# Two hybrid decoder layers on one core: the trunk kept by token instead of by channel

## The chip, the cores and the metric

One NeuronCore of a Trainium2 chip runs the whole program. The metric is device microseconds of one execution. TensorE (PE) multiplies, with a separate record for each load of its stationary operand (PEld); VectorE (DVE), ScalarE (ACT) and GpSimd (POOL) work on vectors; SyncE (SP) issues most DMAs. Products land in PSUM, in banks of 128 partitions by 512 float32.

## The reference

256 tokens of 1024 channels pass through two layers. Each layer is an FFN, a mixer of three attention groups, and a second FFN, each added to the trunk `h`:

```python
for l in range(DEPTH):
    h = h + 0.5 * swiglu(rms_norm(h, ffn1_norm[l]), ffn1_w_gate[l], ffn1_w_up[l], ffn1_w_down[l])
    h = h + hybrid_mixer(rms_norm(h, mix_norm[l]), w_in[l], ...)
    h = h + 0.5 * swiglu(rms_norm(h, ffn2_norm[l]), ffn2_w_gate[l], ffn2_w_up[l], ffn2_w_down[l])
```

`swiglu(x) = (silu(x @ w_gate) * (x @ w_up)) @ w_down` has 2816 hidden channels. The mixer projects the normed trunk once, splits the result into heads of A (four heads over keys that a token indexer selects), B (four heads, causal) and C (eight heads with forget gates), rotates A's and B's queries and keys (rope), and multiplies the heads' outputs by `w_out`.

## The kernel before, in words

**Numbers in two parts.** Each weight and each activation is kept as a high part (rounded to the type fp32r) and a low part (what is left), and a product is made of three: high by high, high by low, low by high (`mm3`, L299). Weights come from HBM in 1 MB raw tiles of five rotating buffers on SP's queue; ACT casts each unit of 1024 columns to the high part (`wh`, L117) and DVE subtracts to get the low part (`wl`, L121). `Weights.pump` (L93) does one such unit ahead of its use; `take` (L133) hands out the next unit, and makes its low part at that point if it isn't there. At most seven units stand ready.

**Order.** The scheduling is by hand: each engine runs its instructions in the order in which the Python code issues them. An engine waits only where a semaphore tells that data or a buffer isn't ready.

**Layout of the trunk.** `hres` (L294) holds the trunk by channel: 128 partitions are channels, in eight slices of 256 tokens. `Norm` (L311) makes from each slice the operand `xhl` with the gains applied: `high` on ACT (L320), `low` on DVE (L323). The squares are taken by ACT (L327), added by POOL and DVE, and summed over partitions by a small TensorE product against ones (`sums`, L341). The root of the mean, by token, is made on POOL (`rsqrt`, L304), turned into a row by a TensorE product (`broadcast`, L348) and multiplied in later, behind the gate products.

**FFN** (L360). In rounds of 128 hidden channels, 22 of them: a gate and an up product (`pair`, L424: each holds 8 weight slices of 128x128 and moves 512 columns of high and low tokens, then 256 of high tokens), then sum, silu and product on ACT and DVE (`summed`, `gated`, `silu`, `hidden`, L439 to L468), which leave the hidden tile as `hh` and `hl`. Four rounds later comes the down product of that tile (`down`, L363). It holds a 128x128 block of weights and moves 256 tokens: 24 products for each hidden tile, into four PSUM banks `acc`, each with two channel slices. The last FFN differs: `turn_trunk` (L381) first transposes the trunk to token by channel, and `down_tokens` (L375) holds 128 tokens of the hidden tile and moves 512 weight columns, 12 products for each hidden tile; `finish` (L391) adds, and stores.

**Boundaries.** `tail` (L518) does the last four hidden tiles (or, in the mixer, the last three head pairs) bank by bank. Behind each bank come the residual addition on DVE (`residual`, L355), and the next norm's highs, lows and squares for its two slices, while TensorE goes on with the next bank. The next FFN begins with a pair in two groups of slices (six, then two), the sums, and the second pair with the broadcast between its wide and narrow products.

**Mixer** (L581). Eight projection chunks of up to 512 columns, each in four steps of two channel slices; they hold tokens and move weight columns. After each step, side work that is due by a step number runs (`at_step`, `run_side`, L585 to L592): rotation, transposes, the indexer, top-k, and B's heads. `post_a` (L800), called behind step 16, evacuates A's chunk and rotates its queries and key on POOL (`rope`, L597); A's root is due at step 22, its split at 24, its transposes at 26. For B's heads (`run_heads`, L917 on) `scores` and `exps` run in one step, `flip` two steps later, which transposes the probabilities and copies them to `pT`, `values` three steps later. A's and C's heads come behind the chunks, with half steps of the output product (`out_halves`) put between their parts.

**Start.** `x` is loaded into `xin`, which takes one of the five raw buffers, turned by TensorE, and the first FFN's first gate product is made slice by slice as it arrives; the turned trunk is then copied to `hres` by ACT and DVE.

Of the kernel before, what the change touches and what calls it, by code (L numbers as in the profile page):

```python
# [18 lines left out]
P = 128  # L19
# [20 lines left out]
B_TURN, B_STEP, A_ROOT, A_TURN, SUMS_STEP = 18, 20, 22, 26, 29  # L40
# [101 lines left out]
def kernel(ctx: ExitStack, tc: tile.TileContext, x, ffn1_norm, ffn1_w_gate, ffn1_w_up, ffn1_w_down,  # L142
# [24 lines left out]
    xin = raw_pool.tile([P, 2048], F32, name="xin", tag="raw").rearrange("p (t d) -> p t d", t=2)  # L167
# [18 lines left out]
    def load_x(mp):  # L186
        cols = slice(256 * mp, 256 * mp + 256)
        nc.sync.dma_start(xin[:, :, cols], x[0].rearrange("(t p) d -> p t d", p=P)[:, :, cols])
# [17 lines left out]
    W.n_raw_done = -1  # L206

# [56 lines left out]
    W.n_raw_done -= RAW_BUFS - 3  # L264
# [8 lines left out]
    W.n_raw_done += RAW_BUFS - 3  # L273
# [20 lines left out]
    hres = xp.tile([P, KT, S], F32, name="hres")  # L294
# [16 lines left out]
    class Norm:  # L311


        def __init__(self, which, l):
            self.col = 16 * which + 8 * l
            self.x = xp.tile([P, KT, 2, S], F32R, name="xhl", tag="xhl")
            self.h, self.l = self.x[:, :, 0], self.x[:, :, 1]
            self.acc = xp.tile([P, 2, S], F32, name="ssacc", tag="ssacc")

        def high(self, m, src=None):  # L320
            A.activation(self.h[:, m], hres[:, m] if src is None else src, AF.Copy, scale=gT[:, self.col + m:self.col + m + 1])

        def low(self, m, src=None):  # L323
            V.scalar_tensor_tensor(self.l[:, m], hres[:, m] if src is None else src, gT[:, self.col + m:self.col + m + 1],
                                   self.h[:, m].bitcast(F32), op0=ALU.mult, op1=ALU.subtract)

        def squares(self, mp):  # L327
            src = hres[:, 2 * mp:2 * mp + 2]
            if mp == 0:
                A.activation(self.acc, src, AF.Square)  # L330
                return
            sq = tmp(512).rearrange("p (a b) -> p a b", a=2)
            A.activation(sq, src, AF.Square)  # L333
            if mp < 3:
                G.tensor_tensor(self.acc, self.acc, sq, op=ALU.add)  # L335
            else:
                V.tensor_tensor(sq[:, 0], sq[:, 0], sq[:, 1], op=ALU.add)
                V.tensor_tensor(sq[:, 0], sq[:, 0], self.acc[:, 0], op=ALU.add)
                V.tensor_tensor(self.acc[:, 0], sq[:, 0], self.acc[:, 1], op=ALU.add)
# [15 lines left out]
    def residual(acc, m, n, factor):  # L355
        V.scalar_tensor_tensor(hres[:, m:m + n], acc[m // 2].rearrange("p (a b) -> p a b", a=2)[:, m % 2:m % 2 + n],
                               factor, hres[:, m:m + n], op0=ALU.mult, op1=ALU.add)


    def ffn(norm, nxt, aside=None, g0=None):  # L360
        hid = {}

        def down(k):  # L363
            w = W.take()
            if nxt is None:
                for j in range(4):
                    down_tokens(j, k, w, slice(0, 512), k == 0, False)
                del hid[k]
                return
# [5 lines left out]
        def down_tokens(j, k, w, cols, start, stop, o=None):  # L375

            t, c = divmod(j, 2)
            mm3(acc[j][:, cols] if o is None else o, [h[:, t * P:(t + 1) * P] for h in hid[k]],
                [v[:, 0, 512 * c + cols.start:512 * c + cols.stop] for v in w], start, stop)

        def turn_trunk():  # L381

            ps = [bank("acc") for _ in range(4)]
            for j in range(4):
                for i in range(4):
                    t, m = j // 2, 4 * (j % 2) + i
                    T.transpose(ps[j][:, i * P:(i + 1) * P], hres[:, m, t * P:(t + 1) * P], ident)
            for j in range(4):
                (A.copy if j % 2 else V.tensor_copy)(trunk[:, j], ps[j])

        def finish(ks):  # L391
            ws = [(k, W.take()) for k in ks]
            dst = out[0].rearrange("(t p) (c d) -> p t c d", p=P, c=2)

            def add(j, cols, ps):
                V.scalar_tensor_tensor(trunk[:, j, cols], ps, 0.25, trunk[:, j, cols], op0=ALU.mult, op1=ALU.add)

            for j in range(4):
                for c in ((0, 512),) if j < 3 else ((0, 256), (256, 512)):
                    c = slice(*c)  # L400
                    o = bank("gu")[:, :S] if c.start else acc[j][:, c]
                    if c.start:
                        add(j, c, acc[j][:, c])
                    for k, w in ws:
                        down_tokens(j, k, w, c, c.start > 0 and k == ks[0], k == ks[-1], o)
                    add(j, c, o)
                    nc.sync.dma_start(dst[:, j // 2, j % 2, c], trunk[:, j, c])

        trunk = hres.rearrange("p a b -> p (a b)").rearrange("p (j c) -> p j c", j=4)
# [14 lines left out]
        def pair(groups=(range(KT),), between=None):  # L424

            ws = [W.take() for _ in range(2)]
            pss = [bank("gu").rearrange("p (a b) -> p a b", a=2) for _ in range(2)]
            for ks in groups:
                for w, ps in zip(ws, pss):
                    for k in ks:  # L430
                        mm(ps, w[0][:, k], norm.x[:, k], k == 0, False)
                if between:
                    between()
                for w, ps in zip(ws, pss):
                    for k in ks:
                        mm(ps[:, 0], w[1][:, k], norm.h[:, k], False, k == KT - 1)
            return pss
# [33 lines left out]
        if first:  # L471
# [4 lines left out]
            for mp in range(1, 4):  # L476
                V.tensor_copy(hres[:, 2 * mp:2 * mp + 2], xT[mp])
# [16 lines left out]
        if nxt is None:  # L494
            turn_trunk()
        acc = [bank("acc") for _ in range(4)]
        for f in range(1, NF):
            last = f == NF - 1
            paired = f >= (PAIR_FROM if first else 2)
            if paired:  # L500
                g, u = pair()
# [16 lines left out]
    def tail(acc, rhs, ks, factor, make_norm, late=None):  # L518


        nxt = make_norm()
        ws = dict(zip(ks, [W.take() for _ in ks]))

        def part(mp, some):
            for k in some:
                for m in (2 * mp, 2 * mp + 1):
                    mm3(acc[mp][:, (m % 2) * S:(m % 2 + 1) * S], [v[:, 0, m * P:(m + 1) * P] for v in ws[k]],
                        rhs[k], False, k == ks[-1])
# [11 lines left out]
        for mp in range(4):  # L540
            ms = (2 * mp, 2 * mp + 1)
            part(mp, ks[ahead[mp]:])
            for m in ms:
                if mp == 3:
                    residual(acc, m, 1, factor)
                elif m == ms[0]:
                    residual(acc, m, 2, factor)
                nxt.high(m)
            if late and mp == 0:
                continue  # L550
            for m in ((0, 1) if late and mp == 1 else ()) + ms:
                nxt.low(m)
            for p in (([0] if late and mp == 1 else []) + ([mp - 1] if mp > 1 or (mp == 1 and not late) else [])
                      + ([3] if mp == 3 else [])):
                nxt.squares(p)
# [25 lines left out]
    def mixer(l, norm, nxt):  # L581
# [218 lines left out]
        def post_a(ps):  # L800
# [5 lines left out]
            for t in range(2):  # L806
# [110 lines left out]
        def run_heads(hs, qk, tag, emit=None, lag=1):  # L917
# [81 lines left out]
            for i, (kind, h) in enumerate(hs):  # L999
                emit(i - 0.5, lambda i=i: (scores(i), exps(i)))  # L1000
# [104 lines left out]
    def turn_x(mp):  # L1105
        ps = bank("acc").rearrange("p (m s) -> p m s", m=2)
        for t in range(2):
            for i in range(2):
                T.transpose(ps[:, i, t * P:(t + 1) * P], xin[:, t, (2 * mp + i) * P:(2 * mp + i + 1) * P], ident)
        xT.append(ps)  # L1110
# [41 lines left out]
    sq = []  # L1152
    for mp in range(4):
        sq.append(norm.acc if mp == 0 else tmp(512).rearrange("p (a b) -> p a b", a=2))
# [52 lines left out]
```

## Time and profile before

| | |
|---|---|
| median of 3 runs | 1053.11 us (1052.83 to 1054.24) |
| profiled execution | 1052.83 us |
| its span, first to last instruction | 1051.0 us |
| granted TensorE clock | 0.999 |
| HBM read | 179.67 MB, 172 GB/s over the span |
| VectorE's largest group, `wl` (L121) | 415.9 us busy, 343 instructions |
| ScalarE's largest group, `wh` (L117) | 345.2 us busy, 343 instructions |

The profile is of one execution. A row of a timeline or of the chain of waits gives the start in us, the time in us, the engine, line and operation with `out<-in`, the shapes (partitions x elements) and how many instructions the row merges; a bracket at its end is idle time of the engine before it, with what ended it. A row of grouped instructions ends in `xcount | busy us, mean ns of one | idle us before them, and what ended it`. A row of waits gives us in total, times and the longest. A row of stretches gives the stretch, its length, then busy us and instructions of PE, PEld, DVE, ACT and POOL, the granted clock, the DMA share and GB/s. Ends of products are modelled, and neighbours overlap; their starts are what the queue shows.

### The profile page before, as it was taken

The page shows a single profiled execution, that of the slowest core. Times are in us where ns is not written, and L with a number is a line of the kernel's source. Part 1 is how long each engine was busy: PE and PEld are TensorE (multiplying, and loading weights), DVE is VectorE, ACT ScalarE, POOL GpSimd, SP SyncE. Part 2 cuts the span into 40 slices and gives each one's busy share as a digit, 9 for nine tenths or more (in the row PEclk, how much of TensorE's full clock was granted, in tenths as well). Part 3 has the DMA queues.
Part 4 walks back from the last instruction along what each step waited for, and adds up shares of the span by engine and source line. Part 5 has one row for each costly group of instructions (what it writes and reads, how often), then busy time and mean ns, then how long its engine had stood idle before and what let it go on. Part 6 is the DMA issues. An engine that isn't in the chain of part 4 may idle for free.

```text
span 1051.0 us, 16911 instructions
## 1 busy us (share of the span) xinstructions
PE 1044.8 (99%) x6611; PEld 948.9 (90%) x6611; DVE 825.6 (79%) x1560; ACT 589.5 (56%) x1026; POOL 162.0 (15%) x184
## 2 busy tenths in 40 slices
PE   9999999999999999999999999999999999999998
PEld 8999999998899899999999999999988998888887
DVE  6997777889876887777788777777898779777775
ACT  6655454666854655454466545546667555554541
POOL 2003000167700100000010210003765000000000
PEclk9999999999999999999999999999999999999999
DMA  9675555365441374555646564645555215564631
GB/s 326 209 240 173 196 197 177 127 218 193 137 148 42 120 241 163 199 182 179 201 161 211 160 238 148 214 145 207 163 181 180 81 41 173 189 232 148 221 120 41
DMA packets 130912, 181.81 MB, mean 173 GB/s; under 512 B 7008, under 2 KB 104720, under 8 KB 130832
## 3 DMA queue, kind: packets, MB, share of 16 engines
q1 hardware_dynamic: 130512, 180.65, 51.5%
q8 instruction: 52, 0.85, 0.3%
q14 instruction: 28, 0.23, 0.1%
q10 hardware_dynamic: 320, 0.08, 0.0%
HBM read 179.67 MB, written 1.05 MB: 172 GB/s over the span
## 4 chain that ended last, share of the span: by engine, by line
PE 93%; DVE 3%; ACT 2%; DMA 1%; issue 0%; SPq 0%; ACTq 0%; DVEq 0%
PE ps_gu L297 61%; PE ps_acc L297 30%; DVE wl L121 1%; ACT wh L117 1%; DMA raw<-in_ffn_w_gate_dram 1%; PE ps_gu L953 1%; PE ps_gu L1053 0%; ACT tmp L615 0%; DMA xin<-in_x_dram 0%; DVE score L754 0%; PE ps_gu L986 0%; DVE tmp L939 0%; DVE tmp L1157 0%; DVE bkT L662 0%; ACT cka L630 0%
## 5 line engine op out<-in xcount | busy, mean ns | idle before, releaser
L121 DVE TENSOR_TENSOR wl<-raw,wh 128x1024 fp32r<-128x1024 f32 (+2 forms) x343 | 415.9, 1219 | 21.4 <-ACT wh L117 21.2
L117 ACT CAST wh<-raw 128x1024 fp32r<-128x1024 f32 (+2 forms) x343 | 345.2, 1035 | 6.6 <-PE ps_gu L297 4.5
L297 PE MATMUL ps_gu<-xhl,wh 128*128 128x512 f32 (+1 forms) x1408 | 336.6, 390 | 0.2 <-DVE tmp L443 0.2
L297 PEld LDWEIGHTS ps_gu<-xhl,wh 128*128 128x128 f32 x1408 | 258.5, 188 | 50.7 <-DVE tmp L443 0.6
L297 PEld LDWEIGHTS ps_gu<-xhl,wl 128*128 128x128 f32 x1400 | 180.6, 191 | 7.2
L297 PE MATMUL ps_gu<-xhl,wl 128*128 128x256 f32 x1400 | 184.1, 283 | 0.0
L443 DVE TENSOR_TENSOR tmp<-ps_gu,tmp 128x256 f32<-128x256 f32 x175 | 73.3, 421 | 108.9 <-ACT tmp L442 108.9
L297 PE MATMUL ps_gu<-wh,xhl 128*128 128x512 f32 (+2 forms) x512 | 158.7, 379 | 0.0
L297 PE MATMUL ps_acc<-hh,wh 128*128 128x256 f32 x528 | 149.4, 283 | 0.0
L297 PE MATMUL ps_acc<-hl,wh 128*128 128x256 f32 x528 | 149.4, 283 | 0.0
L297 PE MATMUL ps_acc<-hh,wl 128*128 128x256 f32 x528 | 149.4, 283 | 0.0
L442 ACT COPY tmp<-ps_gu 128x256 f32<-128x256 f32 x175 | 63.7, 365 | 96.0 <-PE ps_gu L297 95.9
L297 PEld LDWEIGHTS ps_gu<-wh,xhl 128*128 128x128 f32 x512 | 94.9, 188 | 14.4
L457 ACT CAST hh<-tmp 128x256 fp32r<-128x256 f32 x80 | 32.6, 407 | 125.0 <-DVE tmp L454 125.0
L297 PEld LDWEIGHTS ps_acc<-hh,wh 128*128 128x128 f32 x528 | 101.4, 192 | 0.0
L297 PEld LDWEIGHTS ps_acc<-hl,wh 128*128 128x128 f32 x528 | 101.4, 192 | 0.0
L297 PEld LDWEIGHTS ps_acc<-hh,wl 128*128 128x128 f32 x528 | 101.4, 192 | 0.0
L297 PE MATMUL ps_gu<-wl,xhl 128*128 128x512 f32 (+2 forms) x256 | 95.7, 374 | 0.0
L335 POOL TENSOR_TENSOR ssacc<-ssacc,tmp 128x512 f32<-128x512 f32 x10 | 13.0, 1298 | 510.3 <-ACT tmp L333 332.2
L449 ACT ACTIVATE tmp<-tmp 128x256 f32<-128x256 f32 x88 | 36.8, 418 | 83.1 <-DVE tmp L447 83.1
L297 PEld LDWEIGHTS ps_gu<-wl,xhl 128*128 128x128 f32 x256 | 48.2, 188 | 6.5
L454 DVE TENSOR_TENSOR tmp<-tmp 128x256 f32<-128x256 f32 x88 | 37.6, 427 | 3.0
(247 smaller groups left out, 1231.4 us busy)
## 6 DMA issues: line engine op xcount, KB each, us to landing
raw<-in_ffn_w_down_dram SPq DMA_DIRECT2D x44, 1024.0 KB, 5.1
raw<-in_ffn_w_gate_dram SPq DMA_DIRECT2D x43, 1024.0 KB, 7.0
raw<-in_ffn_w_up_dram SPq DMA_DIRECT2D x43, 1024.0 KB, 7.1
raw<-in_w_in_dram SPq DMA_DIRECT2D x24, 1024.0 KB, 5.3
raw<-in_w_out_dram SPq DMA_DIRECT2D x8, 1024.0 KB, 4.8
raw<-in_w_in_dram SPq DMA_DIRECT2D x4, 768.0 KB, 5.2
raw<-in_w_in_dram SPq DMA_DIRECT2D x4, 656.0 KB, 5.2
xin<-in_x_dram SPq DMA_DIRECT2D x4, 256.0 KB, 5.1
```

The costliest lines, as they stand in the source:

```text
L117: self.nc.scalar.copy(hv, src)
L121: (engine or self.nc.vector).tensor_tensor(lv, self.srcs[self.n_low], hv.bitcast(F32), op=ALU.subtract)
L297: T.matmul(o, l, r, start=start, stop=stop, skip_group_check=True)
L335: G.tensor_tensor(self.acc, self.acc, sq, op=ALU.add)
L442: A.copy(o, ps[:, 1])
L443: V.tensor_tensor(o, ps[:, 0], o, op=ALU.add)
L449: A.activation(th, t_, AF.Tanh, scale=0.5)
L454: V.tensor_tensor(t_, u, t_, op=ALU.mult)
L457: (V.tensor_copy if late else A.copy)(hh, t_)
L953: T.transpose(b[:, j * P:(j + 1) * P], pj[i][:, j * P:(j + 1) * P], ident)
```

## The change

1. The trunk is kept by token throughout: `trunk` (128 partitions are tokens, two tiles of 1024 channels) takes the place of `hres` and of `xin`, so that all five raw buffers are free for weights from the start. One raw load therefore moves ahead of the constants and the gains of the mixer and the second FFN on SP's queue.
2. Down and output products have the form of the last FFN everywhere: 512 wide, in four quarters q (two token tiles by two channel halves), 12 for each hidden tile or head pair. `turn_trunk` is gone.
3. At each boundary the trunk is turned by halves (`Norm.half`): eight transposes to two PSUM banks, four highs on ACT and four lows on DVE from PSUM, two squares on ACT. The first half comes behind the third quarter of the tail. The second comes in the next stage: in the mixer behind the first slice of the first chunk, in an FFN behind the first four slices of the first pair's wide products.
4. The FFN's first two pairs are interleaved by halves of the channels; the sums stand behind the first half, the broadcast behind the second pair's wide products.
5. ACT's accumulator sums the squares by token; DVE adds the two halves. POOL's and DVE's additions of squares and TensorE's products against ones are gone.
6. A's rotation is due at steps 18 and 19 instead of right behind step 16. B's `exps` is due one step later than the `scores` of its head, ahead of the next head's `scores`.

```diff
-B_TURN, B_STEP, A_ROOT, A_TURN, SUMS_STEP = 18, 20, 22, 26, 29
+B_TURN, A_ROPE, B_STEP, A_ROOT, A_TURN, SUMS_STEP = 18, 18, 20, 22, 26, 29
...
-    xin = raw_pool.tile([P, 2048], F32, name="xin", tag="raw").rearrange("p (t d) -> p t d", t=2)
+    trunk = xp.tile([P, 2, D], F32, name="trunk")
...
-    W.n_raw_done -= RAW_BUFS - 3
+    W.n_raw_done -= RAW_BUFS - 2
...
-    hres = xp.tile([P, KT, S], F32, name="hres")
...
+            self.ss = sm.tile([P, 4], F32, name="ss4", tag="ss4")
...
+        def turn(self, mp):
+
+            ps = bank("acc").rearrange("p (m s) -> p m s", m=2)
+            for t in range(2):
+                for i in range(2):
+                    T.transpose(ps[:, i, t * P:(t + 1) * P], trunk[:, t, (2 * mp + i) * P:(2 * mp + i + 1) * P], ident)
+            return ps
+
+        def half(self, c):
+
+            ps = [self.turn(2 * c + i) for i in range(2)]
+            srcs = [(4 * c + i, ps[i // 2][:, i % 2]) for i in range(4)]
+            for m, src in srcs:
+                self.high(m, src)
+            for m, src in srcs:
+                self.low(m, src)
+            for t in range(2):
+                self.squares(t, c)
+
+        def squares(self, t, c):
+            A.activation(tmp(512), trunk[:, t, 512 * c:512 * c + 512], AF.Square,
+                         accum_out=self.ss[:, 2 * c + t:2 * c + t + 1])
 
         def sums(self):
-            ss = bank("acc")
-            for t in range(2):
-                mm(ss[:, t:t + 1], self.acc[:, 0, t * P:(t + 1) * P], ones[:, 0:1], t == 0, True)
             a = sm.tile([P, 2], F32, name="msq", tag="msq")
-            self.r = rsqrt(a, ss[:, 0:2], 1.0 / D, 2, "n")
+            V.tensor_tensor(a, self.ss[:, 0:2], self.ss[:, 2:4], op=ALU.add)
+            self.r = rsqrt(a, a, 1.0 / D, 2, "n")
...
+    def tokens(o, q, hid, w, start, stop, cols=slice(0, 512)):
+
+        t, c = q % 2, q // 2
+        mm3(o, [h[:, t * P:(t + 1) * P] for h in hid], [v[:, 0, 512 * c + cols.start:512 * c + cols.stop] for v in w],
+            start, stop)
+
+    def residual(q, ps, factor, cols=slice(0, 512)):
+        t, c = q % 2, q // 2
+        d = trunk[:, t, 512 * c + cols.start:512 * c + cols.stop]
+        V.scalar_tensor_tensor(d, ps, factor, d, op0=ALU.mult, op1=ALU.add)
+        return d
...
         def down(k):
             w = W.take()
-            for m in range(KT):
-                mm3(acc[m // 2][:, (m % 2) * S:(m % 2 + 1) * S],
-                    [v[:, 0, m * P:(m + 1) * P] for v in w], hid[k], k == 0 and m % 2 == 0, False)
+            for q in range(4):
+                tokens(acc[q], q, hid[k], w, k == 0, False)
             del hid[k]
...
-            g0, u0 = pair((range(6), range(6, KT)))
+            lo, hi = range(KT // 2), range(KT // 2, KT)
+            p0, p1 = Pair(), Pair()
+            p0.wide(lo)
+            norm.half(1)
+            p0.narrow(lo)
+            p1.both(lo)
+            W.pump()
             norm.sums()
-            W.pump(2)
+            (g0, u0), (g1, u1) = p0.both(hi), p1.ps
+            W.pump()
             g0, u0 = summed(g0), summed(u0)
             W.pump()
-            g1, u1 = pair(between=norm.broadcast)
+            p1.wide(hi)
+            norm.broadcast()
+            p1.narrow(hi)
             W.pump()
...
+        for q in range(4):
+            part(q, ks[ahead[q]:])
+            residual(q, acc[q], factor)
+            if q == 2:
+                nxt.half(0)
         W.pump()
         return nxt
...
+            def a_rope(t):
                 rope(heads(rot[t], 4), tab[:, 0, 0, t], tab[:, 0, 1, t])
                 rope(ak[t], tab[:, 1, 0, t], tab[:, 1, 1, t])
+
+            for t in range(2):
+                at_step(A_ROPE + t, lambda t=t: a_rope(t))
...
-                emit(i - 0.5, lambda i=i: (scores(i), exps(i)))
+                emit(i - 0.5, lambda i=i: scores(i))
+                emit(i + 0.25, lambda i=i: exps(i))
...
+                    if name == "iq" and k == 0:
+                        norm.half(1)
...
-                    for m in range(4 * hf, 4 * hf + 4):
-                        mm3(acc[m // 2][:, (m % 2) * S:(m % 2 + 1) * S],
-                            [v[:, 0, m * P:(m + 1) * P] for v in w], oT[OUT_ORDER[j]], j == 0 and m % 2 == 0, False)
+                    for q in (2 * hf, 2 * hf + 1):
+                        tokens(acc[q], q, oT[OUT_ORDER[j]], w, j == 0, False)
```

`Pair` has the products of `pair` in two methods, `wide` (512 columns) and `narrow` (256), over any slices.

More of the change, by code (lines that the diff above doesn't have):

```diff
@@ L272 @@
     W.load(1, 1)
[L273 removed]
+    W.n_raw_done += RAW_BUFS - 2
     W.issue()
@@ L391, in finish @@
         def finish(ks):
             ws = [(k, W.take()) for k in ks]
[L393 to L399, printed above, removed]
+            dst = out[0].rearrange("(t p) d -> p t d", p=P)
+            for q in range(4):
+                for c in ((0, 512),) if q < 3 else ((0, 256), (256, 512)):
@@ L409, in ffn @@
-        trunk = hres.rearrange("p a b -> p (a b)").rearrange("p (j c) -> p j c", j=4)
+                        tokens(o, q, hid[k], w, c.start > 0 and k == ks[0], k == ks[-1], c)
+                    d = residual(q, o, 0.25, c)
+                    at = 512 * (q // 2) + c.start
+                    nc.sync.dma_start(dst[:, q % 2, at:at + c.stop - c.start], d)
         def proj(between=None, after=0, tag="gu"):
@@ L500, in ffn @@
             if paired:
-                g, u = pair()
+                g, u = Pair().both()
             else:
@@ L539, in tail @@
             ahead = [2, 2, 1, 0]
[L540 to L555, printed above, removed]
+        for q in range(4):
+            part(q, ks[ahead[q]:])
+            residual(q, acc[q], factor)
+            if q == 2:
+                nxt.half(0)
         W.pump()
@@ L1105, in turn_x @@
     def turn_x(mp):
[L1106 to L1110, printed above, removed]
+        xT.append(norm.turn(mp))
     def gate(w, xs, ks):
@@ L1151 @@
     W.low()
-    sq = []
-    for mp in range(4):
-        sq.append(norm.acc if mp == 0 else tmp(512).rearrange("p (a b) -> p a b", a=2))
-        A.activation(sq[mp], xT[mp], AF.Square)
-    G.tensor_tensor(norm.acc, norm.acc, sq[1], op=ALU.add)
-    add = lambda a, b, o: V.tensor_tensor(o, a, b, op=ALU.add)
-    add(sq[2][:, 0], sq[2][:, 1], sq[2][:, 0])
-    add(sq[3][:, 0], sq[3][:, 1], sq[3][:, 0])
-    add(sq[2][:, 0], sq[3][:, 0], sq[2][:, 0])
-    add(sq[2][:, 0], norm.acc[:, 1], sq[2][:, 0])
-    add(sq[2][:, 0], norm.acc[:, 0], norm.acc[:, 0])
-    A.copy(hres[:, 0:2], xT[0])
+    for c in range(2):
+        for t in range(2):
+            norm.squares(t, c)
     W.high()
     W.low()
-    W.n_raw_done += 1
-    W.issue()
     for l in range(DEPTH):
```

83 lines of the change are left out of this document (21 added, 62 removed).

## The prediction

> **What bounds the kernel now.** I read the page's first part, then the waits of TensorE, then stretches of equal work.
>
> ```profile
> span 1051.0 us, 16911 instructions
> PE 1044.8 (99%) x6611; PEld 948.9 (90%) x6611; DVE 825.6 (79%) x1560; ACT 589.5 (56%) x1026; POOL 162.0 (15%) x184
> ...
> PE ps_gu L297 <- POOL minus_half L183: 1.0, 1, 1.0
> PE ps_acc L297 <- ACT pT L955: 0.8, 2, 0.4
> PE ps_acc L1109 <- DMA xin<-in_x_dram: 0.4, 1, 0.4
> PE ps_acc L297 <- DVE ssacc L1157: 0.3, 1, 0.3
> ```
>
> TensorE (PE) is busy for 99% of the span, and all that it waits for by name is some 2.7 us. VectorE (DVE) has a fifth of its time free, ScalarE (ACT) nearly half. So the time is the length of TensorE's queue of products, one after the other. An edit counts by what it adds to or takes from that queue, and by any new wait; work on other engines counts only if TensorE comes to wait for it. "Busy" alone does not give the price of a product, since neighbours overlap. I take prices from start to start.
>
> **The down products.** The last FFN already computes them as the changed kernel does everywhere: hidden tile stationary, 512 weight columns moving. The other FFNs hold 128x128 weights and move 256 tokens. So the trace has both forms in the same loop. The view by stretches gives 16 rounds of each (a pair of gate and up products, then one down step):
>
> ```profile
> 374.95:510.09 135.14, 135.14 (x897) 124.79 (x897) 101.25 (x162) 71.10 (x117) 0.00 (x0) 1.00 0.58 193
> 895.63:1028.22 132.59, 132.59 (x706) 114.76 (x705) 100.41 (x162) 70.39 (x114) 0.00 (x0) 1.00 0.52 174
> ```
>
> 135.14 / 16 = 8.446 us against 132.59 / 16 = 8.287: 0.159 us less for each round, at a granted clock of 1.00 in both. One down step alone, from the chain of waits (first row) and TensorE's timeline:
>
> ```profile
> 372.07 2.88 PE ps_acc L297 x24
> ...
> 892.88 0.40 PE L297 MATMUL ps_acc<-wh,hh 128*128 128x512 f32 x1
> 893.12 0.40 PE L297 MATMUL ps_acc<-wl,hh 128*128 128x512 f32 x1
> ...
> 895.63 3.79 PE L297 MATMUL ps_gu<-xhl,wh 128*128 128x512 f32 x16
> ```
>
> 24 products of 256 take 2.88 us (0.120 each); 12 of 512 take 895.63 - 892.88 = 2.75 (0.229 each, the first 0.24). The counts:
>
> ```profile
> L297 PE MATMUL ps_acc<-hh,wh 128*128 128x256 f32 x528 | 149.4, 283 | 0.0
> L297 PE MATMUL ps_acc<-hl,wh 128*128 128x256 f32 x528 | 149.4, 283 | 0.0
> L297 PE MATMUL ps_acc<-hh,wl 128*128 128x256 f32 x528 | 149.4, 283 | 0.0
> ```
>
> 3 x 528 = 1584 = 66 steps of 24. At 0.159 a step, **-10.5 us**. The output product has 8 steps in each of two layers. It does not run in rounds with pairs, so I take 2.88 - 2.75 = 0.13 to 0.159 a step and choose 0.15: **-2.4 us**. Ends for both together: 82 steps at 0.13 and at 0.159, -10.7 and -13.0.
>
> By the Trainium skill (TensorE: Matmul & The Clock Gate, "Back-to-back issue gap") a warm product costs N/2.4 + 2.5 ns, 109.2 for 256 columns and 215.8 for 512, so a join saves 2.5 ns; as an estimate, 984 joins would save 2.5 us and the whole sum below would end at +2.1 us. By that rule the change loses; the trace disagrees, with 120 and 229 ns.
>
> **The turns.** The trunk now lies by token, and each of five boundaries (two FFN to mixer, two mixer to FFN, one FFN to FFN) turns it with 16 transposes in two groups of 8 (Norm.half). The one turn of before, ahead of the last FFN, shows the price:
>
> ```profile
> 874.41 1.91 PE L387 MATMUL ps_acc<-cst,hres 128*128 128x128 f32 x16
> 876.07 3.92 PE L297 MATMUL ps_gu<-xhl,wh 128*128 128x512 f32 x16
> 879.84 2.08 PE L297 MATMUL ps_gu<-xhl,wl 128*128 128x256 f32 x16
> 881.75 3.82 PE L297 MATMUL ps_gu<-xhl,wh 128*128 128x512 f32 x16
> 885.40 2.08 PE L297 MATMUL ps_gu<-xhl,wl 128*128 128x256 f32 x16
> ```
>
> 16 transposes hold the queue for 876.07 - 874.41 = 1.66 us, and the 16 products behind them take 3.77 against 3.65 in the next round (885.40 - 881.75): 0.12 for the switch. A group of 8 is 0.83 + 0.12 = 0.95, ten of them **+9.5 us** (ends: 8.3 without a switch, 10.7 with two per group). The old turn goes: 1.66 + 0.12, **-1.8 us**. Its copies (two on DVE, two on ACT) go too; they were off the path.
>
> By the Trainium skill (same page, "Part 4: PE-mode transpose") a transpose takes some 275 ns in a kernel and does not keep the clock up; at 275 ns each the ten groups would be an estimated 23 us and the sum +5. The trace disagrees on what the queue pays: 1.66 / 16 = 104 ns from start to start.
>
> **The sums of squares.** They were four records of tiny products per norm on TensorE; ACT's accumulator now makes them:
>
> ```profile
> 348.68 0.57 PE L297 MATMUL ps_acc<-ones,ssacc 128*128 128x1 f32 x4
> 349.11 3.90 PE L297 MATMUL ps_gu<-xhl,wh 128*128 128x512 f32 x16
> 352.84 0.61 PE L297 MATMUL ps_acc<-cst,y_n 128*128 128x128 f32 x4
> ...
> 202.97 0.50 PE L297 MATMUL ps_acc<-ones,ssacc 128*128 128x1 f32 x4
> 203.33 0.48 PE L297 MATMUL ps_gu<-wh,xhl 128*128 128x512 f32 x1
> ...
> 16.52 0.99 PE L297 MATMUL ps_gu<-xhl,wl 128*128 128x256 f32 x7
> 17.84 0.58 PE L297 MATMUL ps_acc<-ones,ssacc 128*128 128x1 f32 x4 [0.32 <-DVE ssacc L1157]
> 18.27 0.37 PE L297 MATMUL ps_gu<-xhl,wl 128*128 128x256 f32 x1
> ```
>
> Into an FFN: 0.43, and 352.84 - 349.11 = 3.73 for the next 16, 0.08 over 3.65: 0.51, three times. Into a mixer: 0.36 and about 0.09 of switch: 0.45, twice. In the first FFN 18.27 - 16.52 = 1.75, of which 7 x 0.120 = 0.84 are products: 0.91. Sum **-3.3 us**. ACT's accumulating square is not in the trace: it costs ACT between the present square and one more small read, and it stands behind the highs, not ahead of a product, so 0 on the path (bounds 0 to +0.5). DVE's three and POOL's two adds per boundary go, also 0.
>
> **Side work.** The exponentials of B now stand one step later in ACT's queue, behind the copy of pT instead of ahead of it. TensorE's wait of 0.8 us for pT arises because ACT stands in front of an exponential:
>
> ```profile
> 263.72 0.40 ACT L946 ACTIVATE p<-tmp,nm 128x128 f32<-128x128 f32 x1 [0.61 <-DVE nm L939]
> ...
> 244.87 0.64 POOL L603 TENSOR_TENSOR swapped<-aqr,tab 128x128 f32<-128x128 f32 x1
> 257.27 0.32 POOL L606 TENSOR_TENSOR ak<-ak,swapped 128x64 f32<-128x64 f32 x1
> 265.09 2.87 POOL L308 TENSOR_TENSOR y_a<-ssa,minus_half 128x10 f32<-128x10 f32 x1 [7.50 <-DVE ssa L307]
> ```
>
> I count **-0.8 us** (bounds 0 and -1.1). A's rotation takes POOL 257.59 - 244.87 = 12.7 us, and POOL then idles 7.5 us before A's root. Issued two and three steps later (a step of 12 products of 512 is 12 x 0.229 = 2.75 us), it still ends some 2 us before the root starts if the first half is issued 5.5 us later and the second follows: 0, with 0 to +1 as bounds, since the split that reads it comes two steps behind the root. At the start one 1 MB load moves ahead of the constants and two gain loads on SP's queue; these are first read behind FFN round 8: 0.
>
> **New waits.** After each group of 8, ACT makes four highs and DVE four lows before the products that read them:
>
> ```profile
> L321 ACT ACTIVATE xhl<-ps_acc,gT 128x256 fp32r<-128x256 f32 x8 | 3.4, 471 | 0.2
> L324 DVE SCALAR_TENSOR_TENSOR xhl<-ps_acc,gT,xhl 128x256 fp32r<-128x256 f32 x8 | 3.5, 479 | 2.4 <-ACT xhl L321 2.4
> L356 DVE SCALAR_TENSOR_TENSOR hres<-ps_acc,hres 128x512 f32<-128x512 f32 x15 | 10.3, 687 | 4.8 <-PE ps_acc L297 4.8
> L121 DVE TENSOR_TENSOR wl<-raw,wh 128x1024 fp32r<-128x1024 f32 x327 | 402.1, 1235 | 21.4 <-ACT wh L117 21.2
> ```
>
> From the group's start: first bank turned at about 0.6 us, first low at 0.6 + 0.47 + 0.48 = 1.6, the last three highs later, at 3.0. First half: the last quarter's products cover it (mixer 9 x 0.229 = 2.05, FFN 12 x 0.229 = 2.75, behind 0.95 of transposes): 3.0 and 3.7, so the first low has 1.4 us to spare. Second half: its transposes need the last residual (0.69), covered by 8 products (1.8) or, in the mixer, 6 (1.4); its lows may stand behind one or two subtractions of 1.2 and still have 3.7 us of products in front. What is late next is the third pair of the FFN: it needs the bank of the second pair's up half, which DVE frees at the end of a chain that begins with the broadcast root. The FFN behind an FFN:
>
> ```profile
> 541.29 0.42 DVE L447 TENSOR_TENSOR tmp<-tmp,rb 128x256 f32<-128x256 f32 x1
> 548.53 0.42 DVE L443 TENSOR_TENSOR tmp<-ps_gu,tmp 128x256 f32<-128x256 f32 x1
> ...
> 547.48 3.82 PE L297 MATMUL ps_gu<-xhl,wh 128*128 128x512 f32 x16
> ```
>
> Bank free at 548.95, wanted at 547.48 + 8 x 0.229 = 549.3: 0.35 to spare. Before, the broadcast stands behind a pair (3.65 + 1.91 = 5.56), the sums (0.5) and 3.65 of the next pair: 9.7 us into the FFN. Now it stands behind a pair, a turn (0.95), half a pair (2.79) and 1.82: 11.1, so 1.4 later, while the third pair comes only 0.45 later (0.95 less 0.5). 1.4 - 0.45 - 0.35 = 0.6 us of wait here; behind a mixer I estimate 0.2, twice: **+1.0 us** (bounds 0 and 5, one per boundary).
>
> **Sum**: -10.5 - 2.4 + 9.5 - 1.8 - 3.3 - 0.8 + 1.0 = -8.3 us. The profiled execution took 1052.83 us, 1.8 beyond its span and 0.3 below the median of 1053.11; I forecast **1044.5**.
>
> **Rivals.**
> - *Waits at the turns* (slower). The highs queue behind weight casts and the lows behind subtractions, so the turn's chain comes out on TensorE. The sum has 9.3 us to lose without its +1.0; over five boundaries the change breaks even at 1.9 us each. The first low would have to come 1.4 + 1.9 = 3.3 us late, three subtractions of 1.2 in front of it. For: the FFN puts three there at its end. Against: the turn comes two quarters behind them. With 2.4 us at each, -9.3 + 12.0 = +2.7: 1055.5. Chance 6%.
> - *The join saves nothing*: every product of 512 takes the 0.24 of the first, as 2 x 0.120. Then -8.3 + 12.9 = +4.6: 1057.4. Against it stands the last FFN's 8.287. The skill's gap rule is of this kind. 3%.
> - *Partial waits*: 1 us or more at each boundary or a late third pair in all three FFNs, 3 to 6 us: 1047.5 to 1051. 13%.
> - *The change does not do what it says for B*: pT stays late, or A's later rotation delays its split: 0.8 to 1.8 back, within my range.
> - Gain and waits cancel, 1051.0 to 1055.2: 8%.
>
> **Numbers.** My case, 1041.5 to 1047.5, has 69%; its lower end takes -13.0 for the joins, 8.3 for the groups, -1.1 for pT and no wait (-10.9). With the partial waits the range is 1041.5 to 1050. Below it 1%. About 0.2% (2.1 us) is what a measurement of this kernel can tell from no change. Faster by more: 69 + 13 + 1 = 83%. Within: 8%. Slower: 9%.
>
> **What would show it.** Right: a round of 8.29 us in all four FFNs; ten groups of transposes at 0.95 from start to next product; no row of ssacc; named waits of TensorE below 4 us; no wait on pT. Wrong: rounds near 8.45, a wait on xhl behind a turn, a wait on tmp at the third pair of over 1 us, or a granted clock below 1.0 behind the transposes.

## The result and the profile after

The changed kernel takes 1044.55 us (median of 4 runs, 1043.99 to 1044.97) against 1052.97 (4 runs, 1052.66 to 1054.24): a ratio of 0.9917 (0.99 to 0.9935), 8.4 us less. The forecast was 1044.5. The profiled execution of the changed kernel took 1044.58 us. Its page, first part:

```profile
span 1042.8 us, 15029 instructions
...
PE 1036.8 (99%) x5667; PEld 900.4 (86%) x5667; DVE 810.9 (78%) x1536; ACT 588.8 (56%) x1047; POOL 143.5 (14%) x173
```

TensorE still fills 99% of the span, now with 5667 products instead of 6611: the time came out of TensorE's queue, as the busy time shows (1044.8 to 1036.8). Its waits by name, in total us, times and the longest:

```profile
PE ps_gu L294 <- DVE tmp L435: 1.2, 3, 0.6
PE ps_gu L294 <- POOL minus_half L183: 1.0, 1, 1.0
PE ps_acc L329 <- DMA trunk<-in_x_dram: 0.3, 1, 0.3
```

The waits for `pT` and for the sums of squares are gone. One has grown: 1.2 us on `tmp` at L435, where DVE adds the two halves of a product and so frees its bank. Of these, 0.2 us near the start stood in the kernel before too (`PE ps_gu L297 <- DVE tmp L443: 0.2, 1, 0.2`).

16 rounds of the second and of the third FFN, in the view by stretches (columns as before):

```profile
372.40:504.99 132.59, 132.59 (x706) 114.76 (x705) 101.72 (x163) 71.18 (x116) 0.00 (x0) 1.00 0.58 197
557.60:690.23 132.63, 132.63 (x706) 114.81 (x705) 102.69 (x163) 71.15 (x116) 9.05 (x16) 1.00 0.59 199
```

Each round takes 132.59 / 16 = 8.287 us, where it took 8.446: both FFNs have the rounds that only the last one had. The groups of instructions show the transposes (count, busy us, mean ns):

```profile
L329 PE MATMUL ps_acc<-cst,trunk 128*128 128x128 f32 x96 | 13.3, 279 | 0.3 <-DMA trunk<-in_x_dram 0.3
```

The 96 transposes are the 16 at the start and ten groups of 8. TensorE's timeline at the boundary from FFN to FFN shows two of these groups, and the third pair:

```profile
521.28 1.03 PE L329 MATMUL ps_acc<-cst,trunk 128*128 128x128 f32 x8
522.07 0.48 PE L294 MATMUL ps_acc<-wh,hh 128*128 128x512 f32 x1
522.38 0.40 PE L294 MATMUL ps_acc<-wl,hh 128*128 128x512 f32 x1
522.62 0.39 PE L294 MATMUL ps_acc<-wh,hl 128*128 128x512 f32 x1
...
524.88 1.98 PE L294 MATMUL ps_gu<-xhl,wh 128*128 128x512 f32 x8
526.71 1.03 PE L329 MATMUL ps_acc<-cst,trunk 128*128 128x128 f32 x8
527.50 1.20 PE L294 MATMUL ps_gu<-xhl,wl 128*128 128x256 f32 x8
528.53 2.00 PE L294 MATMUL ps_gu<-xhl,wh 128*128 128x512 f32 x8
...
542.92 2.00 PE L294 MATMUL ps_gu<-xhl,wh 128*128 128x512 f32 x8
545.34 1.88 PE L294 MATMUL ps_gu<-xhl,wh 128*128 128x512 f32 x7 [0.41 <-DVE tmp L435]
```

A group holds the queue for 522.07 - 521.28 = 0.79 us, and the first product behind it takes 522.38 - 522.07 = 0.31 where its neighbour takes 0.24. The second group is the same: 0.79, then 1.03 for eight narrow products that take 0.96 without it. With the switch a group costs about 0.88. In the last row the up half of the third pair waits: 545.34 - 542.92 = 2.42 for eight products of 0.23, so 0.57 too long. The bracket shows only 0.41, since the record of a product runs on beyond the start of the next. The eight products behind the wait take 547.28 - 545.34 = 1.94 instead of 1.83, so over the whole pair it costs 0.70.

Where the 8.25 us between the two spans' ends came from, stage by stage. A stage begins with its first gate or projection product in TensorE's timeline; the first begins and the last ends with the span. The fourth column adds up the prediction's terms that fall into the stage:

| stage | before, us | after, us | change | predicted |
|---|---|---|---|---|
| first FFN, with the start | 197.50 | 194.87 | -2.63 | -3.46 |
| first mixer | 145.56 | 145.25 | -0.31 | -0.15 |
| second FFN | 186.84 | 184.76 | -2.08 | -1.91 |
| third FFN | 186.71 | 185.27 | -1.44 | -1.51 |
| second mixer | 145.64 | 145.23 | -0.41 | -0.15 |
| last FFN | 188.79 | 187.41 | -1.38 | -1.14 |

Five stages agree within 0.3 us. The first FFN lacks 0.8. Its place is in round 9, in TensorE's timeline of the changed kernel:

```profile
74.11 0.29 PE L177 MATMUL ps_gu<-cst,tmp 16*128 16x16 f32 x2
74.33 2.11 PE L294 MATMUL ps_gu<-xhl,wh 128*128 128x512 f32 x8
77.04 2.11 PE L294 MATMUL ps_gu<-xhl,wh 128*128 128x512 f32 x8 [0.61 <-DVE tmp L435]
```

and of the kernel before, where the same products follow without a gap:

```profile
75.72 0.29 PE L177 MATMUL ps_gu<-cst,tmp 16*128 16x16 f32 x2
75.94 3.82 PE L297 MATMUL ps_gu<-xhl,wh 128*128 128x512 f32 x15
```

The up half starts 77.04 - 74.33 = 2.71 behind the gate half, 0.78 more than the 1.93 that eight products take right behind small ones (experiment 4 has a row of that). What it waits for, in DVE's timeline after and before:

```profile
69.70 0.42 DVE L435 TENSOR_TENSOR tmp<-ps_gu,tmp 128x256 f32<-128x256 f32 x1
...
76.57 0.42 DVE L435 TENSOR_TENSOR tmp<-ps_gu,tmp 128x256 f32<-128x256 f32 x1
```

```profile
77.41 0.42 DVE L443 TENSOR_TENSOR tmp<-ps_gu,tmp 128x256 f32<-128x256 f32 x1
```

The turning of the gains (L177) sits behind round 8 and takes two of the rotating banks, so the up half of round 9 needs the bank that held the up half of round 8. DVE frees it at 76.57 + 0.42 = 76.99, and before at 77.83, just ahead of 75.94 + 1.93 = 77.87, when it was wanted. TensorE came to this place 74.33 against 75.94, 1.61 us earlier; DVE came 0.84 earlier. DVE is late in this FFN: its sums of the up half are 76.57 - 69.70 = 6.87 us apart, less than a round of 8.29, so it is still catching up.

The first gate product also starts 7.66 - 7.42 = 0.24 us later than before. In the profiled executions of the experiments, which leave the start as it is, it starts at 7.47 to 9.66 us, so whether the change has a part in the 0.24 cannot be told from one execution of the kernel before.

### The profile page after: what moved, and what is told of

Its sections match the earlier page's. It is cut to its first block, busy times and chain, and to the rows that moved or that the text cites. A ratio compares the mean times of both kernels' runs of the same rounds, so it can differ in the third digit from the quotient of the medians.

```text
span 1042.8 us, 15029 instructions
## 1 busy us (share of the span) xinstructions
PE 1036.8 (99%) x5667; PEld 900.4 (86%) x5667; DVE 810.9 (78%) x1536; ACT 588.8 (56%) x1047; POOL 143.5 (14%) x173
## 4 chain that ended last, share of the span: by engine, by line
PE 92%; DVE 4%; ACT 2%; DMA 1%; issue 1%; SPq 0%; ACTq 0%
PE ps_gu L294 61%; PE ps_acc L294 28%; ACT wh L117 2%; DVE wl L121 1%; PE ps_acc L329 1%; DVE tmp L435 1%; PE ps_gu L943 1%; DMA trunk<-in_x_dram 1%; PE ps_gu L1045 1%; DVE tmp L459 0%; DVE tmp L446 0%; DVE tmp L439 0%; DVE tmp L458 0%; PE ps_acc L644 0%; ACT tmp L434 0%
## 5 line engine op out<-in xcount | busy, mean ns | idle before, releaser
L294 PEld LDWEIGHTS ps_gu<-xhl,wh 128*128 128x128 f32 x1408 | 261.4, 188 | 55.5 <-DVE tmp L435 2.9
L435 DVE TENSOR_TENSOR tmp<-ps_gu,tmp 128x256 f32<-128x256 f32 x175 | 73.6, 421 | 105.1 <-ACT tmp L434 104.9
L294 PE MATMUL ps_acc<-wh,hh 128*128 128x512 f32 (+1 forms) x352 | 137.7, 391 | 0.0
L294 PE MATMUL ps_acc<-wl,hh 128*128 128x512 f32 (+1 forms) x352 | 137.4, 390 | 0.0
L294 PE MATMUL ps_acc<-wh,hl 128*128 128x512 f32 (+1 forms) x352 | 136.5, 388 | 0.0
L305 POOL TENSOR_TENSOR y_n<-msq,minus_half 128x2 f32<-128x2 f32 x6 | 7.7, 1280 | 540.4 <-DVE msq L304 540.4
L294 PEld LDWEIGHTS ps_acc<-wh,hl 128*128 128x128 f32 x352 | 66.1, 188 | 14.1
L294 PEld LDWEIGHTS ps_acc<-wh,hh 128*128 128x128 f32 x352 | 66.4, 189 | 11.7
L294 PEld LDWEIGHTS ps_acc<-wl,hh 128*128 128x128 f32 x352 | 66.4, 189 | 10.8
L318 ACT ACTIVATE xhl<-ps_acc,gT 128x256 fp32r<-128x256 f32 x48 | 19.0, 474 | 37.5 <-PE ps_acc L329 37.0
```

Source lines behind the costliest of these rows:

```text
L294: T.matmul(o, l, r, start=start, stop=stop, skip_group_check=True)
L305: G.tensor_tensor(y, dst, minus_half[:, :n], op=ALU.pow)
L318: A.activation(self.h[:, m], src, AF.Copy, scale=gT[:, self.col + m:self.col + m + 1])
L435: V.tensor_tensor(o, ps[:, 0], o, op=ALU.add)
```

## The experiments

All change the kernel after. Each states its time (median, and range of the timed runs) and its ratio to the kernel before with the interval; "the control" is the kernel after, run again.

### 1. The down and output products cut in two

```diff
-        mm3(o, [h[:, t * P:(t + 1) * P] for h in hid], [v[:, 0, 512 * c + cols.start:512 * c + cols.stop] for v in w],
-            start, stop)
+        for a in range(0, cols.stop - cols.start, 256):
+            at = 512 * c + cols.start + a
+            mm3(o[:, a:a + 256], [h[:, t * P:(t + 1) * P] for h in hid], [v[:, 0, at:at + 256] for v in w],
+                start and a == 0, stop)
```

> The changed kernel, with each 512-wide down and output product cut into two of 256 columns; operands, order and layout as in the changed kernel. Theory (the join is worth 0.13 to 0.159 us a step on TensorE's queue): 82 steps come back, and here also the last FFN's 22, which were 512 wide before: 104 steps, 13.5 to 16.5 us more than the changed kernel's 1044.55, so 1058.1 to 1061.1. Rival (the gain came from waits or from another operand being held, not from the width): within 2 us of 1044.6. By the Trainium skill's gap formula (TensorE: Matmul & The Clock Gate, Back-to-back issue gap) a join is worth 2.5 ns: as an estimate, 1248 of them would be 3.1 us, 1047.7.

1059.53 us (1059.37 to 1059.72), ratio 1.0061 (1.0046 to 1.0076): 15.0 more than after, and slower than before. Its chain of waits:

```profile
376.34 5.57 PE ps_gu L294 x32
381.90 2.88 PE ps_acc L294 x24
384.78 5.57 PE ps_gu L294 x32
```

The round is 384.78 - 376.34 = 8.44 again, with trunk, turns and order of the changed kernel; only the width differs. The waits say what else moved:

```profile
PE ps_gu L294 <- DVE tmp L437: 0.6, 2, 0.4
```

The wait of round 9 is gone, since TensorE comes later to it. So the 104 steps cost at most 15.0 + 0.78 = 15.8, or 0.152 each. In the profiled executions 0.63 us of this lie ahead of the first gate product (8.29 against 7.66), which leaves 15.2, or 0.146 each. The width is where the gain comes from.

### 2. Every transpose of the boundaries twice

```diff
-        def turn(self, mp):
+        def turn(self, mp, times=1):
...
-                    T.transpose(ps[:, i, t * P:(t + 1) * P], trunk[:, t, (2 * mp + i) * P:(2 * mp + i + 1) * P], ident)
+                    for _ in range(times):
+                        T.transpose(ps[:, i, t * P:(t + 1) * P], trunk[:, t, (2 * mp + i) * P:(2 * mp + i + 1) * P], ident)
...
-            ps = [self.turn(2 * c + i) for i in range(2)]
+            ps = [self.turn(2 * c + i, 2) for i in range(2)]
```

> The changed kernel, with every transpose of a boundary's turn made twice into the same place (80 transposes more; the outcome is unchanged). Theory (a turn costs its time in TensorE's queue, 0.79 us for eight, and hides nothing else): ten groups, 7.9 us more than 1044.55, so 1052.5, and no new named wait of TensorE. Rival (the turn's chain through ScalarE and VectorE comes out on TensorE, so a later turn costs more than its own length): over 10 us more, 1055 and above, with waits on xhl. Rival (transposes run in the shadow of their neighbours): under 3 us more.

1053.31 us (1053.03 to 1053.69), ratio 1.0002 (0.9993 to 1.0011): 8.8 more than after. Its timeline at the boundary from FFN to FFN:

```profile
524.83 1.91 PE L330 MATMUL ps_acc<-cst,trunk 128*128 128x128 f32 x16
526.49 0.48 PE L294 MATMUL ps_acc<-wh,hh 128*128 128x512 f32 x1
526.80 0.40 PE L294 MATMUL ps_acc<-wl,hh 128*128 128x512 f32 x1
```

16 hold the queue for 526.49 - 524.83 = 1.66 instead of 0.79, ten times 0.87 = 8.7, and the switch behind them is paid once as before (0.31). The wait on `tmp` stays at 1.2 us in three. So the turns cost TensorE their own time and nothing hides them: they are the price against which the joins pay.

### 3. The first half turned behind the last quarter

```diff
-            if q == 2:
+            if q == 3:
                 nxt.half(0)
```

> The changed kernel, with the first half's turn behind the last quarter of the tail instead of behind the third, so that no products stand between its transposes and the products that read its highs and lows. Theory (2.05 to 2.75 us of the last quarter hide the chain, of which the first low takes 1.6 us and the fourth 3.0 from the first transpose, and 0.79 of that are transposes): an FFN's first products wait about 0.8 us and go on at the pace of the highs, 3 x 0.4 against 3 x 0.23, so some 1.4 us at each of three boundaries into an FFN; into a mixer, where a slice takes 1.4 us, some 0.9 at each of two: 6 us more than 1044.55, 1050.5, with TensorE waiting on xhl by name. The second half's turn stands right behind and may share part of it: 4 to 8 more. Rival (the cover is not needed, VectorE keeps up anyway): under 1.5 us more.

1051.99 us (1051.53 to 1053.45), ratio 0.9991 (0.9981 to 1.0): 7.4 more than after, nearly the whole gain. The new wait:

```profile
PE ps_gu L294 <- DVE xhl L321: 3.3, 5, 1.0
```

One at each of the five boundaries. Its timeline at FFN to FFN:

```profile
528.33 1.04 PE L329 MATMUL ps_acc<-cst,trunk 128*128 128x128 f32 x8
530.39 2.67 PE L294 MATMUL ps_gu<-xhl,wh 128*128 128x512 f32 x8 [1.01 <-DVE xhl L321]
532.90 1.04 PE L329 MATMUL ps_acc<-cst,trunk 128*128 128x128 f32 x8
```

Behind the transposes 530.39 - 528.33 - 0.79 = 1.27 us pass until the first slice is there, and the eight products that follow take 532.90 - 530.39 = 2.51 instead of 526.71 - 524.88 = 1.83, each waiting a little for its low: 1.95 less 0.08 for the switch. Three FFNs at 1.87 and, by the same reckoning, two mixers at 0.83 give 7.3 of the 7.4. The first low is there 530.39 - 528.33 = 2.06 us after the group's start, later than the 1.6 of the prediction, so what it had to spare behind a mixer's tail in the changed kernel was 0.9 and not 1.4. The last quarter covers this chain; without it the chain comes out on TensorE.

### 4. Small products for the sums put back

```diff
         def sums(self):
+            ps = bank("acc")
+            for t in range(2):
+                mm(ps[:, t:t + 1], trunk[:, t, 0:P], ones[:, 0:1], t == 0, True)
```

> The changed kernel, with two tiny products of a 128x128 piece of the trunk against a column of ones put back into TensorE's queue where each norm's sums stand; nothing reads them. Theory (0.45 to 0.51 us for each norm, with the switch between forms): six norms, 2.4 to 3.1 us more than 1044.55, so 1047.0 to 1047.6. Rival (they fall into gaps of the queue): under 0.8 us more.

1047.19 us (1047.15 to 1047.38), ratio 0.9944 (0.993 to 0.9959): 2.6 more than after. The products' result is not used, so nothing waits for it. Timeline of the second FFN's beginning:

```profile
347.27 0.51 PE L294 MATMUL ps_acc<-ones,trunk 128*128 128x1 f32 x4
347.63 2.08 PE L294 MATMUL ps_gu<-xhl,wh 128*128 128x512 f32 x8
349.56 0.64 PE L294 MATMUL ps_gu<-xhl,wl 128*128 128x256 f32 x4
```

Four products of one column hold the queue for 347.63 - 347.27 = 0.36, and the eight behind them take 349.56 - 347.63 = 1.93 instead of 1.83: 0.46, in six places 2.8, against 2.6 measured.

### 5. The control

> The changed kernel once more, as it is, as the mark for the three beside it: 1044.5, within 0.7 us.

1044.63 us (1044.48 to 1044.9), ratio 0.9922 (0.9908 to 0.9936).

### 6. B's exponentials back behind their scores

```diff
-                emit(i - 0.5, lambda i=i: scores(i))
-                emit(i + 0.25, lambda i=i: exps(i))
+                emit(i - 0.5, lambda i=i: (scores(i), exps(i)))
```

> The changed kernel, with B's exponentials again right behind their scores in ScalarE's queue. Theory (the copy of pT stands behind an exponential that waits for VectorE): TensorE's wait for pT is back by name, 0.4 us in each layer, 0.8 to 1.1 us more than the changed kernel beside it, 1045.4. Rival (the wait went because A's rotation moved, or because the turn gave VectorE time): no wait for pT, no difference.

1045.76 us (1045.53 to 1046.68), ratio 0.9935 (0.9922 to 0.9947): 1.13 more than the control. The wait is back, in the list of waits

```profile
PE ps_acc L294 <- ACT pT L945: 0.8, 2, 0.4
```

and in TensorE's timeline of the first mixer:

```profile
262.40 0.62 PE L294 MATMUL ps_acc<-bkT,bqT 128*128 128x128 f32 x4
263.43 0.88 PE L294 MATMUL ps_acc<-va,pT 128*128 128x65 f32 x6 [0.42 <-ACT pT L945]
```

263.43 - 262.40 = 1.03, where the kernel after has

```profile
261.68 0.62 PE L294 MATMUL ps_acc<-bkT,bqT 128*128 128x128 f32 x4
262.13 0.78 PE L294 MATMUL ps_acc<-va,pT 128*128 128x65 f32 x6
```

0.45: 0.58 in each mixer, 1.16 in both. The six products behind the wait also take 0.72 instead of 0.62.

### 7. A's rotation back behind step 16

```diff
             for t in range(2):
-                at_step(A_ROPE + t, lambda t=t: a_rope(t))
+                a_rope(t)
```

> The changed kernel, with A's rotation again right behind step 16. Theory (GpSimd idles some 7 us before A's root, and nothing reads the rotation before that): no difference over 0.4 us to the changed kernel beside it; VectorE's subtractions and scores near step 17 take longer beside the rotation. Rival (the later rotation is what frees VectorE in time for B): 0.8 us or more added, with a wait of TensorE for bkT or pT.

1044.96 us (1044.62 to 1045.13), ratio 0.9924 (0.9911 to 0.9938): 0.33 more than the control, with overlapping ranges. In the profiled executions the first mixer takes the same time (145.23 us), and 0.35 of the 0.5 us by which the spans differ lie ahead of the first gate product. So where the rotation stands is worth nothing that these runs can tell.

### 8. Without the two waits for a bank

The gains are turned behind round 12 instead of round 8. In the later FFNs the broadcast stands ahead of the second pair's last wide products, and one more weight unit is cast ahead of adding up the first pair's halves (`summed`) instead of behind it.

```diff
-            W.pump()
+            W.pump(2)
             g0, u0 = summed(g0), summed(u0)
-            W.pump()
-            p1.wide(hi)
             norm.broadcast()
+            p1.wide(hi)
             p1.narrow(hi)
...
-            if f == 8 and aside:
+            if f == 12 and aside:
```

> The changed kernel without what makes its two longest new waits: the side work that turns two gain rows (two banks of the gate and up products) stands behind FFN round 12 instead of 8; and in the later FFNs the broadcast of the root stands ahead of the second pair's last wide products, with one weight cast ahead of the sums instead of behind. Theory (TensorE waits 0.77 us in round 9 since the two small transposes shift the banks while VectorE is still behind, and 0.57 us at the third pair of the FFN behind an FFN, since VectorE frees the up half's bank late): both go, 1.3 us less than the changed kernel beside it, 1043.2. Rival (the waits only move to a later round, as VectorE's chain stays as long): the same time, with a wait on tmp elsewhere.

1042.57 us (1042.5 to 1043.22), ratio 0.9904 (0.989 to 0.9917): 2.06 less than the control, and faster than both kernels. From its waits:

```profile
PE ps_gu L294 <- DVE tmp L435: 0.2, 1, 0.2
```

Of the control's 1.3 us on `tmp` this is left. Round 9 of the first FFN and the third pair behind the boundary, in its timeline:

```profile
73.93 3.79 PE L294 MATMUL ps_gu<-xhl,wh 128*128 128x512 f32 x16
77.56 2.08 PE L294 MATMUL ps_gu<-xhl,wl 128*128 128x256 f32 x16
...
541.76 3.82 PE L294 MATMUL ps_gu<-xhl,wh 128*128 128x512 f32 x16
545.41 2.08 PE L294 MATMUL ps_gu<-xhl,wl 128*128 128x256 f32 x16
```

77.56 - 73.93 = 3.63 and 545.41 - 541.76 = 3.65: no gap in either. Against the control the first FFN is 0.85 us shorter, the three others 0.22, 0.72 and 0.22. Over whole pairs, from the first of the 16 wide products to the first narrow one, the control loses 4.72 - 3.76 = 0.96 in round 9 (3.76 is what a pair takes here behind the same two gain rows, after round 12), 4.36 - 3.65 = 0.71 in the third pair behind the FFN, and 3.89 - 3.65 = 0.24 in each of the two third pairs behind a mixer. That is 2.15 together, the whole of the 2.06: the waits go and do not move to a later round. The expected 1.3 had counted the two longest gaps alone.

Round 9's wait is set by the gains' place. At the third pair the edit moves two things, the broadcast and a cast, and this run does not tell them apart. In the trace of the kernel after both are at work. ACT has the root's row ready (`rb`, L357) at 536.60 + 0.38 = 536.98; on DVE stand

```profile
535.07 2.35 DVE L121 TENSOR_TENSOR wl<-raw,wh 128x1024 fp32r<-128x1024 f32 x2
537.34 0.42 DVE L439 TENSOR_TENSOR tmp<-tmp,rb 128x256 f32<-128x256 f32 x1
```

DVE uses the row first at 537.34, behind two subtractions of weights.

## Why the prediction was right, step by step

The forecast was 1044.5, measured 1044.55; the mechanism of every larger step is shown. Some sizes were off, and the errors nearly cancel.

- **Down and output products, -10.5 and -2.4.** The mechanism is right, and so is the first size; the second is too large. The rounds have the predicted 8.287. Of the 0.159 that a round gains, 0.133 lie in the down products and 0.027 in the 16 wide products behind them, which take 3.627 instead of 3.654 us. The 16 output steps take 46.40 instead of 47.97 us from start to start: -1.6, or 0.10 a step, below the 0.13 that the prediction took as the least; why, no run tells. Undone alone, a step is worth 0.146 on average (experiment 1), so 82 steps are -12.0 of the -12.9. In the tails, where no pair stands between, a down step gains a little less than the 0.159 taken from the rounds, as the chains of before and after show at the end of the second FFN:

```profile
515.66 14.40 PE ps_acc L297 x120
```

```profile
510.53 10.91 PE ps_acc L294 x48
```

  14.40 / 5 = 2.88 against 10.91 / 4 = 2.73: 0.15. The "joins save nothing" rival is out.

  By the Trainium skill's formula for the spacing of isolated products (TensorE: Matmul & The Clock Gate, "Back-to-back issue gap": N/2.4 + 2.5 ns), which the page itself sets apart from a stream of weight loads and products, experiment 1 would have cost an estimated 3 us. It cost 15, and the measurement decides.
- **Turns, +9.5.** Mechanism right, size 0.7 too high: a group costs 0.88, not 0.95. The 0.83 was half of a row of 16; eight hold the queue for 0.79, and the switch is 0.08 for a group, not 0.12. Experiment 2 gives ten times 0.87, and the queue pays 0.79 / 8 = 99 ns a transpose from start to start, at a mean duration of 279. The granted clock stayed at 1.00 around the transposes, with twice as many of them too (experiment 2).

  The Trainium skill (same page, "Part 4: PE-mode transpose") states some 275 ns. The traces agree with it as a duration; as a price in the queue, an estimated 22 us in experiment 2, it is far off.
- **Sums of squares, -3.3.** About right: 2.6 by experiment 4, which doesn't bring back the wait on DVE in the first FFN. That wait was 0.3 us by its bracket and 17.84 - 16.52 - 0.84 = 0.5 from start to start: 3.1 together.
- **The exponentials, -0.8 (bounds 0 and -1.1).** Right in place, too small in size: the wait is 0.58 in each mixer instead of 0.4 (experiment 6), and between before and after the scores' and value products lose 0.68 and 0.65 in the two mixers, 1.3 together. The bracket of a wait falls short of what the queue loses; from start to start is the price. The 1.13 of experiment 6 lies just past the bound.
- **A's rotation, 0.** Right within 0.4 (experiment 7).
- **New waits, +1.0.** The third pair behind the FFN waits 0.57 (0.70 over the whole pair), predicted 0.6, for the predicted bank. Behind the mixers it was 0.2 twice; the timeline of the second FFN shows it without a bracket:

```profile
358.16 4.02 PE L294 MATMUL ps_gu<-xhl,wh 128*128 128x512 f32 x16
362.01 2.08 PE L294 MATMUL ps_gu<-xhl,wl 128*128 128x256 f32 x16
```

  362.01 - 358.16 = 3.85 against 3.65: 0.2. In the last FFN it is 877.27 - 873.42 = 3.85, the same. What the prediction did not see is 0.78 us in round 9 of the first FFN. It took TensorE's faster rounds there as pure gain, and did not ask whether DVE, which is behind in that FFN, keeps up where an extra pair of banks is taken. Experiment 8 shows it by moving that pair.
- **Waits at the turns (the slower rival).** It did not come: no wait on `xhl` is in the list. Experiment 3 shows that its mechanism is real, with 1.9 us at an FFN once the cover of one quarter is gone, as much as the prediction named as break-even for each boundary.

Together with the measured sizes: -12.0 + 8.8 - 1.8 - 3.1 - 1.3 + 1.9 = -7.5, where the waits are 0.7 + 0.2 + 0.2 at the third pairs and 0.8 in round 9. The old turn's -1.8 is the prediction's own; its row is gone, but it was not tried by itself. The spans give -8.25, so 0.7 is not placed term by term. By kind of product nothing is left over. This table adds up, over the whole of both traces, the time from each product's start to the next one's:

| products | before, us | after, us | change |
|---|---|---|---|
| down | 250.54 | 241.77 | -8.77 |
| output | 47.97 | 46.40 | -1.57 |
| gate, up and projection, with their waits and switches | 657.81 | 657.31 | -0.50 |
| transposes of `x` and of the trunk | 3.79 | 10.02 | +6.23 |
| sums of squares | 2.39 | 0 | -2.39 |
| all others, B's heads and the start among them | 83.93 | 82.80 | -1.13 |

That is -8.13; the other 0.12 lies behind the last product. The near hit is in part luck: 0.7 too much for the turns and 0.5 too little for the exponentials stand against 0.8 too much gain from the output products and 0.8 for a wait that was missed.

## What to carry to other kernels

When one engine's queue is the time, price each edit from start to start in that queue, with a row of the same form in the same kind of loop; durations and brackets of idle time mislead both ways. A turn between layouts pays if it is bought once per boundary and the wider products come many times, and if other products stand behind it while its operands are made. Where the bounding engine gets faster, look at each place that takes extra buffers and ask whether the engine that frees them was only just in time before.

## What the runs showed of the hardware

ACT's square with an accumulator is two instructions. ACT's timeline at the boundary from FFN to FFN:

```profile
523.36 0.65 ACT L344 ACTIVATE tmp<-trunk 128x512 f32<-128x512 f32 x1
523.88 0.22 ACT L344 ACTIVATION_READ_ACCUMULATOR tmp<-trunk 128x1 f32 x1
523.97 0.64 ACT L344 ACTIVATE tmp<-trunk 128x512 f32<-128x512 f32 x1
```

The read is 0.22 us by its record, but the next square starts 523.97 - 523.36 = 0.61 behind the first. Plain squares of this size in the kernel before (L333) follow each other by 0.52, so the read costs some 0.09 on ACT's queue, less than half of its record. And TensorE pays about 0.08 us on top (0.07 to 0.11) each time the queue goes from transposes or from one-column products back to products of 256 or 512 columns, in every place looked at.
